# A decoder layer on one core: gated branch results summed by accumulating transfers, and a third staging buffer

## The chip, the core and the metric

The kernel runs on one core of a Trainium2 chip. Its engines are called here as in the profile: PE (TensorE, the matmuls), PEld (its weight loads), DVE (VectorE), ACT (ScalarE), POOL (GpSimd) and SP (SyncE, which issues nearly all transfers here). Each engine, and the queue of transfers that it issues, works through its own program in order. The metric is the device time of one execution in microseconds (us).

## The reference

One decoder layer over 1024 tokens of width 1024, all in float32: token mixing by three branches, then cross-attention into a memory of 256 rows, then an MLP with squared ReLU, and a final norm. What matters here is the end of the mixing:

```python
g = jax.nn.sigmoid(gates.reshape(bn, s_len, N_BRANCH, D_MODEL))
merged = (g[:, :, 0] * (od @ w_branch[l, 0])
          + g[:, :, 1] * (o_r @ w_branch[l, 1])
          + g[:, :, 2] * (o_l @ w_branch[l, 2]))
x = x + merged @ w_out[l]
```

`od`, `o_r` and `o_l` are the results of differential attention, retention and the recurrent unit. Each branch is a product of 1024x1024 by 1024x1024, gated by a sigmoid per element, and the three are added.

## The kernel before, in words

Every float32 operand of a matmul is split into two fp32r parts: `split` (L68) casts the high part on ACT (L70) and subtracts on DVE or POOL for the low part (L71). A product is then three matmuls per block, hi-hi, hi-lo, lo-hi (L59 to L61).

The large products run by Strassen's scheme in Winograd's form: seven products of half-size blocks in place of eight. `product` (L1104) makes one: it splits a weight block on ACT and DVE or POOL (tile `wu`), runs twelve matmuls into one of six PSUM buffers (tag `p`), and passes the sums that are complete on to `emit`. The sums of weights that the scheme needs are formed by `left` (L1064) on DVE in the staging tiles `st` and `sf`.

`branch` (L792) is called three times by `run` (L1302 to L1304), in the order retention, attention, recurrent; `order` counts the calls, `i` is the branch. In each call the first two pairs of weight units (p = 0, 1) run one after the other, and the last two (p = 2, 3) interleaved, product by product, so that the seven blocks of the activations come free one by one. While that goes on, `load_blocks` (L755) and `fill_block` (L770) refill each freed block with a block of the next branch's activations: two halves of 512 KB each are loaded into a staging tile `st2` (pool `bst`, two buffers, L1301; the profile calls it `st`) and split on ACT and DVE. In the third call there is no next branch: the merged sums are split into `mT` for the output projection, the first half of the rows read back from DRAM through the same staging buffers (L836), the second half straight from SBUF (L816).

`emit` (L800) handles one result tile of 128x512, 16 per call. It loads the gate tile `sg` (L803, four buffers; the profile calls it `sgb`), takes the sigmoid on ACT (L804), and from the second call on loads the running sum `pv` of the calls before (L807, three buffers). On DVE it adds the two parts of the product into `y` (L809, three buffers), multiplies by the gate (L810), and adds `pv` (L812). SP then stores `y` in a DRAM tensor (L814), one for each call (`self.acc`, L148), except for the last eight tiles of the third call.

The order of the instructions on each engine and queue is set by a scheduler when the program is built. A tile's buffer is taken again when its last reader is done; for `y` that reader is the transfer that stores it.

Of the kernel before, what the change touches and what calls it, by code (L numbers as in the profile page):

```python
# [9 lines left out]
F32 = mybir.dt.float32  # L10
F32R = mybir.dt.float32r
AF = mybir.ActivationFunctionType
ALU = mybir.AluOpType
# [4 lines left out]
P = 128  # L18
S = 1024
D = 1024  # L20
KT = 8
HB = 512
# [13 lines left out]
def f32(ap):  # L36
    return ap.bitcast(F32)
# [12 lines left out]
class Kernel:  # L50
# [85 lines left out]
    def setup(self):  # L136
        nc, tc, a, ctx = self.nc, self.tc, self.a, self.ctx
        self.const = ctx.enter_context(tc.tile_pool(name="const", bufs=1))
        self.small = ctx.enter_context(tc.tile_pool(name="small", bufs=4))
        self.stage = ctx.enter_context(tc.tile_pool(name="stage", bufs=3))  # L140
        self.wpool = ctx.enter_context(tc.tile_pool(name="wpool", bufs=4))
        self.dram = ctx.enter_context(tc.tile_pool(name="dram", bufs=1, space=DRAM))
        self.ps = ctx.enter_context(tc.tile_pool(name="ps", bufs=2, space=PSUM))
        dr = lambda n, shape: self.dram.tile(shape, F32, name=n)
        self.orT, self.odT, self.olT = dr("orT", [D, S]), dr("odT", [D, S]), dr("olT", [D, S])
        self.rows = dr("rows", [16, HB])
        self.onT, self.hTs = dr("onT", [D, S]), dr("hTs", [4, P, 4, HB])
        self.acc = [dr(f"acc{i}", [D, S]) for i in range(3)]  # L148
        self.oTs = [dr(f"oTs{i}", [4, P, 4, HB]) for i in range(3)]
        self.gsp = dr("gsp", [3 * D, S])  # L150
        self.h1 = self.dram.tile([8, 7, P, 2, HB], F32, name="h1")
        self.x2, self.x3 = dr("x2", [S, D]), dr("x3", [S, D])

        self.cm = cm = self.const.tile([P, 4, P], F32, name="cm")
        self.ident, self.ones, self.tril, self.negm = (cm[:, i, :] for i in range(4))
        self.onesr = self.const.tile([P, P], F32R, name="onesr")
        self.mhalf = self.const.tile([P, 8], F32, name="mhalf")
        nc.gpsimd.memset(self.mhalf, -0.5)
        self.vec = self.const.tile([P, NV], F32, name="vec")
        self.eps5 = self.const.tile([P, 1], F32, name="eps5")  # L160
        nc.gpsimd.memset(self.eps5, 1e-5)
        nc.scalar.activation(self.small.tile([P, 1], F32, tag="ss", name="ss", bufs=4), self.eps5, AF.Square)
        z = f32(self.wpool.tile([P, 2, D], F32R, tag="w", name="w"))[:, 0, 0:HB]
        nc.vector.memset(z, 0.0)
        for _ in range(3):
            nc.tensor.matmul(self.ps.tile([P, HB], F32, tag="mm", name="mm"), lhsT=z[:, 0:P], rhs=z, start=True, stop=True)
# [480 lines left out]
    def h_products(self):  # L647
# [64 lines left out]
        for p in range(2):  # L712
            run(p, 1)
            yield
# [8 lines left out]
        for k in self.BY_BLOCK[1:]:  # L723
            for p in range(2):
                run(p, k)
        for p in range(2, m - 2):
            for k in self.ORDER:
                run(p, k)
# [63 lines left out]
    def branch(self, order, i, right, bw, st, sps, nxt):  # L792

        nc, v = self.nc, self.nc.vector
        tile = lambda: st.tile([P, 2, HB], F32, tag="st2", name="st2")
        after, load = (None, None) if nxt is None else self.load_blocks(nxt, tile)
        mT = [[None, None], [None, None]]
        cs = [{} for _ in range(4)]

        def emit(n, j, x, y):  # L800
            rows, sl = slice(n * P, (n + 1) * P), slice(j * HB, (j + 1) * HB)
            sg = bw.tile([P, HB], F32, tag="sg", name="sgb", bufs=4)
            nc.sync.dma_start(sg, self.gsp[i * D + n * P:i * D + (n + 1) * P, sl])  # L803
            nc.scalar.activation(sg, sg, AF.Sigmoid)  # L804
            if order > 0:
                pv = bw.tile([P, HB], F32, tag="pv", name="pv", bufs=3)
                nc.sync.dma_start(pv, self.acc[order - 1][rows, sl])  # L807
            o = bw.tile([P, HB], F32, tag="y", name="y", bufs=3)
            v.tensor_tensor(o, x, y, op=ALU.add)  # L809
            v.tensor_tensor(o, o, sg, op=ALU.mult)  # L810
            if order > 0:
                v.tensor_tensor(o, o, pv, op=ALU.add)  # L812
            if nxt is not None or n < 4:
                nc.sync.dma_start(self.acc[order][rows, sl], o)  # L814
            else:
                self.split(mT[j][1][:, n % 4, :], o)  # L816

        def run(p, k):
            units = [self.a["w_br"][i * 8 + 2 * p + e] for e in range(2)]
            self.pair(p, k, cs[p], units, right, self.p6(sps), lambda e, j, x, y: emit(2 * p + e, j, x, y),  # L820
                      v if k in (6, 4) else nc.gpsimd)

        for p in range(2):
            for k in self.BY_BLOCK:
                run(p, k)
        for k in self.BY_BLOCK:
            for p in (2, 3):
                run(p, k)
            if nxt is not None:
                next(load)  # L830
            elif k in (1, 3):
                mT[k // 2][1] = self.block(self.slotA)
            elif k in (2, 7):
                j = 1 - k // 4
                mT[j][0] = self.block((self.slotB, self.slotA)[j])
                x = self.acc[2][:, j * HB:(j + 1) * HB].rearrange("(k p) c -> p k c", p=P)  # L836
                self.fill_block(mT[j][0], x, tile)
        return mT if nxt is None else after

# [445 lines left out]
    def run(self):  # L1285
        tc, nc, a = self.tc, self.nc, self.a
        pool = lambda name, bufs=1, side="right", **kw: tc.tile_pool(name=name, bufs=bufs, side=side, reuse_waits="tile", **kw)
        self.setup()
        with pool("slotA", bufs=4, side="left") as self.slotA:
# [5 lines left out]
            with pool("slotB", bufs=4) as self.slotB:  # L1295
                with pool("sps", space=PSUM) as sps:
                    with pool("sp") as self.sp:
                        self.sps = sps
                        for _ in self.hp:
                            pass  # L1300
                    with pool("bst", bufs=2) as st, pool("bw") as bw:  # L1301
                        right = self.branch(0, 1, self.right, bw, st, sps, 0)  # L1302
                        right = self.branch(1, 0, right, bw, st, sps, 2)
                        mT = self.branch(2, 2, right, bw, st, sps, None)  # L1304
# [94 lines left out]
```

## Time and profile before

| | |
|---|---|
| median of 3 runs | 2452.02 us (2450.01 to 2455.37) |
| the profiled execution | 2450.84 us, span 2448.9 us, mean granted clock 0.985 |
| PE busy | 2312.1 us, 94% of the span |
| DVE, ACT, POOL busy | 1885.1 (77%), 1043.4 (43%), 997.8 us (41%) |
| transfers | 338.27 MB, mean 138 GB/s |
| the merge of the three branches | some 1262 to 1536 us of the span |

The span is from the first to the last instruction. Busy times overlap between engines. The granted clock is TensorE's, as a share of 2.4 GHz. A wait is put down to what ended it last. In the rows below, "x2" means that two like instructions are merged, and their time is the sum.

### The profile page before, as it was taken

What the parts mean: (1) busy time and instruction counts of PE and PEld (TensorE: products, weight loads), DVE (VectorE), ACT (ScalarE), POOL (GpSimd) and SP (SyncE); (2) the same over time, 40 slices, a digit from 0 to 9 for tenths busy, and PEclk for the clock granted to TensorE, in tenths of its full rate; (3) what the DMA queues carried; (4) which work ended last, traced back from release to release, by engine and by line L of the source; (5) the groups of instructions that cost most, each with busy time, mean ns of one, the idle gap of its engine ahead of it and who ended that gap; (6) DMA issues with size and microseconds to landing.
All of it is one profiled execution on the core that took longest, in us unless ns stands there. A gap on an engine that the chain in (4) does not pass through costs nothing.

```text
span 2448.9 us, 31204 instructions
## 1 busy us (share of the span) xinstructions
PE 2312.1 (94%) x11132; PEld 1901.4 (78%) x11132; DVE 1885.1 (77%) x2920; ACT 1043.4 (43%) x1823; POOL 997.8 (41%) x644
## 2 busy tenths in 40 slices
PE   9999999999999989899998988999989999899996
PEld 7888878888887867677877766788768888778884
DVE  7677387877797787897787888345788888788888
ACT  5444355555555444545244444135432222343333
POOL 1122212221215434455422214034155555698787
PEclk9999999999999999999999989999999999999999
DMA  4222222222225345443576785343324443734431
GB/s 172 80 86 70 65 61 70 66 61 65 61 51 186 123 153 189 144 159 131 193 257 224 249 281 183 112 163 104 113 83 166 152 160 135 276 136 173 160 137 73
DMA packets 137258, 338.27 MB, mean 138 GB/s; under 512 B 17152, under 2 KB 27393, under 8 KB 137104
## 3 DMA queue, kind: packets, MB, share of 16 engines
q1 hardware_dynamic: 136528, 334.44, 41.5%
q8 instruction: 89, 1.46, 0.3%
q10 hardware_dynamic: 576, 1.84, 0.2%
q14 instruction: 65, 0.53, 0.1%
HBM read 229.21 MB, written 98.63 MB: 134 GB/s over the span
## 4 chain that ended last, share of the span: by engine, by line
PE 51%; DVE 20%; DMA 11%; issue 8%; POOL 5%; ACT 4%; SPq 0%; DVEq 0%; POOLq 0%; ACTq 0%
PE ps L61 7%; PE ps L59 7%; PE ps L60 7%; POOL wu L71 3%; PE psq L59 2%; PE psq L61 2%; PE psq L60 2%; PE sc L458 2%; PE psk L61 2%; DVE block L71 2%; PE psk L60 2%; PE psk L59 2%; DVE acc L1199 2%; DMA st<-oTs 1%; PE psv L60 1%
## 5 line engine op out<-in xcount | busy, mean ns | idle before, releaser
L59 PE MATMUL ps<-block,wu 128*128 128x512 f32 x1428 | 567.6, 398 | 48.3 <-DVE sf L1126 16.1
L61 PE MATMUL ps<-block,wu 128*128 128x512 f32 x1428 | 564.8, 396 | 22.3 <-DVE wu L71 15.2
L60 PE MATMUL ps<-block,wu 128*128 128x512 f32 x1428 | 560.7, 393 | 0.2 <-DVE block L71 0.2
L71 POOL TENSOR_TENSOR wu<-st,wu 128x512 fp32r<-128x512 f32 x144 | 226.0, 1577 | 385.4 <-ACT wu L70 341.8
L59 PEld LDWEIGHTS ps<-block,wu 128*128 128x128 f32 x1428 | 271.0, 190 | 111.9 <-ACT wu L70 29.0
L61 PEld LDWEIGHTS ps<-block,wu 128*128 128x128 f32 x1428 | 270.5, 189 | 90.5 <-DVE wu L71 18.6
L60 PEld LDWEIGHTS ps<-block,wu 128*128 128x128 f32 x1428 | 270.8, 190 | 60.0 <-DVE block L71 1.1
L70 ACT CAST wu<-st 128x512 fp32r<-128x512 f32 x240 | 141.3, 618 | 156.7 <-DVE st L1066 63.1
L59 PE MATMUL ps<-wu,hu 128*128 128x512 f32 x448 | 177.2, 395 | 16.9 <-DVE acc L1199 14.1
L71 POOL TENSOR_TENSOR w<-st,w 128x1024 fp32r<-128x1024 f32 x50 | 124.7, 2505 | 161.3 <-ACT w L70 161.3
L61 PE MATMUL ps<-wu,hu 128*128 128x512 f32 x448 | 174.7, 392 | 3.8 <-DVE hu L71 3.8
L60 PE MATMUL ps<-wu,hu 128*128 128x512 f32 x448 | 175.5, 392 | 0.0
L1199 DVE TENSOR_TENSOR acc<-acc,ps 128x512 f32<-128x512 f32 x216 | 137.8, 677 | 20.5 <-PE ps L61 20.0
L71 POOL TENSOR_TENSOR wu<-sf,wu 128x512 fp32r<-128x512 f32 x63 | 116.3, 1859 | 53.5 <-ACT wu L70 51.7
L71 DVE TENSOR_TENSOR hu<-sth,hu 128x1024 fp32r<-128x1024 f32 x56 | 121.1, 2167 | 20.4 <-ACT hu L70 19.9
L466 ACT ACTIVATE p<-sc,mx 128x256 f32<-128x256 f32 (+7 forms) x128 | 94.8, 741 | 69.9 <-DVE mx L463 50.2
L71 DVE TENSOR_TENSOR wu<-st,wu 128x512 fp32r<-128x512 f32 x96 | 90.1, 954 | 35.1 <-ACT wu L70 35.1
L59 PEld LDWEIGHTS ps<-wu,hu 128*128 128x128 f32 x448 | 84.6, 189 | 40.8 <-DVE acc L1199 12.2
L61 PEld LDWEIGHTS ps<-wu,hu 128*128 128x128 f32 x448 | 84.7, 189 | 22.9 <-DVE hu L71 5.1
L59 PE MATMUL psk<-block,w 128*128 128x512 f32 x256 | 102.2, 399 | 0.0
L61 PE MATMUL psk<-block,w 128*128 128x512 f32 x256 | 101.4, 396 | 0.0
L60 PE MATMUL psk<-block,w 128*128 128x512 f32 x256 | 101.3, 396 | 0.0
(389 smaller groups left out, 5638.5 us busy)
## 6 DMA issues: line engine op xcount, KB each, us to landing
sth<-h SPq DMA_DIRECT2D x56, 512.0 KB, 9.5
st<-in_w SPq DMA_DIRECT2D x32, 512.0 KB, 4.3
h<-hab SPq DMA_DIRECT2D x32, 512.0 KB, 2.8
w<-in_w SPq DMA_DIRECT2D x8, 2048.0 KB
sgb<-gsp SPq DMA_DIRECT2D x48, 256.0 KB, 4.6
gsp<-l SPq DMA_DIRECT2D x44, 256.0 KB, 4.0
acc<-y SPq DMA_DIRECT2D x40, 256.0 KB, 4.1
st<-in_w_br SPq DMA_DIRECT2D x18, 512.0 KB, 5.9
```

The lines of the kernel that those rows point to most:

```text
L59: nc.tensor.matmul(ps, lhsT=lhs.hi, rhs=rhs.hi, start=start, stop=False)
L60: nc.tensor.matmul(ps, lhsT=lhs.hi, rhs=rhs.lo, start=False, stop=False)
L61: nc.tensor.matmul(ps, lhsT=lhs.lo, rhs=rhs.hi, start=False, stop=stop)
L70: ins = self.nc.scalar.copy(dst.hi, src)
L71: self.lo_ins = (lo_engine or self.nc.vector).tensor_tensor(dst.lo, src, f32(dst.hi), op=ALU.subtract)
L458: nc.tensor.matmul(sc[:, b * HB:b * HB + e], lhsT=qt[:, c, part, cols], rhs=k[b][:, c, 0:e], start=part == 0, stop=part == 1)
L466: nc.scalar.activation(p[:, 0:n], sc[:, 0:n], AF.Exp, bias=mx, accum_out=l)
L1199: eng.tensor_tensor(acc[k][:, st, :], acc[k][:, st, :], x if isinstance(x, bass.AP) else acc[x][:, st, :], op=ALU.add)
```

## The change

The three DRAM tensors for the running sum become one. In the first call SP stores each result there as before. In the second call, and for the first eight results of the third, a transfer issued by POOL adds the result to what stands in DRAM (`accum_op=ALU.add`); the load of `pv` and the addition on DVE are gone there. The last eight results of the third call load the sum and add it as before. The gate tile has three buffers in place of four, `pv` two in place of three, and the staging pool of `fill_block` three in place of two; the room in SBUF is the same.

```diff
-        self.acc = [dr(f"acc{i}", [D, S]) for i in range(3)]
+        self.acc = dr("acc", [D, S])
...
-            sg = bw.tile([P, HB], F32, tag="sg", name="sgb", bufs=4)
+            sg = bw.tile([P, HB], F32, tag="sg", name="sgb", bufs=3)
             nc.sync.dma_start(sg, self.gsp[i * D + n * P:i * D + (n + 1) * P, sl])
             nc.scalar.activation(sg, sg, AF.Sigmoid)
-            if order > 0:
-                pv = bw.tile([P, HB], F32, tag="pv", name="pv", bufs=3)
-                nc.sync.dma_start(pv, self.acc[order - 1][rows, sl])
+            acc, last = self.acc[rows, sl], nxt is None and n >= 4
+            if last:
+                pv = bw.tile([P, HB], F32, tag="pv", name="pv", bufs=2)
+                nc.sync.dma_start(pv, acc)
             o = bw.tile([P, HB], F32, tag="y", name="y", bufs=3)
             v.tensor_tensor(o, x, y, op=ALU.add)
             v.tensor_tensor(o, o, sg, op=ALU.mult)
-            if order > 0:
+            if not last:
+                if order == 0:
+                    nc.sync.dma_start(acc, o)
+                else:
+                    nc.gpsimd.dma_start(acc, o, accum_op=ALU.add)
+            else:
                 v.tensor_tensor(o, o, pv, op=ALU.add)
-            if nxt is not None or n < 4:
-                nc.sync.dma_start(self.acc[order][rows, sl], o)
-            else:
                 self.split(mT[j][1][:, n % 4, :], o)
...
-                x = self.acc[2][:, j * HB:(j + 1) * HB].rearrange("(k p) c -> p k c", p=P)
+                x = self.acc[:, j * HB:(j + 1) * HB].rearrange("(k p) c -> p k c", p=P)
...
-                    with pool("bst", bufs=2) as st, pool("bw") as bw:
+                    with pool("bst", bufs=3) as st, pool("bw") as bw:
```

PE's program is the same before and after. On the other engines the scheduler moves instructions in this stage; three places follow. Numbers are buffer numbers, and an arrow points from what is read to what is written.

SP's queue in the second call, while p = 0 and p = 1 run (before; `acc_79` is the running sum being written, `acc_78` the one read):

```order
L814 DMA acc_79<-y 128x512
L807 DMA pv<-acc_78 128x512
L1077 DMA st<-in_w_br 128x1024
L774 DMA st_13026<-olT 128x2x512
L774 DMA st_13030<-olT 128x2x512
L803 DMA sgb<-gsp 128x512
```

And with the change, at the end of the first call and the start of the second:

```order
L774 DMA st_12659<-oTs_79 128x1024
L774 DMA st_13000<-olT 128x2x512
L814 DMA acc<-y 128x512 x3
L803 DMA sgb<-gsp 128x512 x3
L1080 DMA st<-in_w_br 128x1024
L803 DMA sgb<-gsp 128x512
L1080 DMA st<-in_w_br 128x1024
L774 DMA st_13004<-olT 128x2x512
L774 DMA st_13054<-olT 128x2x512
```

The first load of the next branch's block (`st_13000<-olT`) now stands ahead of the last stores of the first call, so three are issued ahead and not two, and no store or load of the sum is left between the loads of weights, gates and blocks.

POOL's queue, from the end of the second call to p = 1 of the third (before), where `wu` are weight splits:

```order
L71 TENSOR_TENSOR wu_13466<-sf_8246,wu_13466 128x512
L71 TENSOR_TENSOR wu_13577<-st_13528,wu_13577 128x512
L71 TENSOR_TENSOR wu_13577<-sf_8246,wu_13577 128x512
L71 TENSOR_TENSOR wu_13608<-sf_8246,wu_13608 128x512
L71 TENSOR_TENSOR wu_13755<-st_13688,wu_13755 128x512
```

The same place with the change:

```order
L71 TENSOR_TENSOR wu_13413<-sf_8244,wu_13413 128x512
L816 DMA acc_78<-y_13251 128x512
L816 DMA acc_78<-y_13282 128x512
L816 DMA acc_78<-y_13305 128x512
L816 DMA acc_78<-y_13357 128x512
L71 TENSOR_TENSOR wu_13512<-st_13466,wu_13512 128x512
L71 TENSOR_TENSOR wu_13512<-sf_8244,wu_13512 128x512
L71 TENSOR_TENSOR wu_13543<-sf_8244,wu_13543 128x512
L816 DMA acc_78<-y_13432 128x512
L816 DMA acc_78<-y_13440 128x512
L816 DMA acc_78<-y_13462 128x512
L816 DMA acc_78<-y_13504 128x512
```

The transfers stand in groups of two to four between the splits; the results of p = 0 of the third call (from `y_13432` on) come behind the three splits of p = 1.

DVE in the third call, p = 0 and the first result of p = 1 (before: L809 adds, L810 multiplies, L812 adds the running sum, L1066 forms the weight sums that the splits of p = 1 read):

```order
L809 TENSOR_TENSOR y_13523<-ps1_13505,sf_8246 128x512
L812 TENSOR_TENSOR y_13498<-y_13498,pv_13496 128x512
L810 TENSOR_TENSOR y_13523<-y_13523,sgb_13518 128x512
L1066 TENSOR_TENSOR st_13528<-sf_8246,st_13528 128x512
L812 TENSOR_TENSOR y_13523<-y_13523,pv_13521 128x512
L809 TENSOR_TENSOR y_13568<-ps1_13550,sf_8246 128x512
L1066 TENSOR_TENSOR st_13528<-st_13528 128x512
```

With the change (the lines are L810, L811 and L1069 there):

```order
L1069 TENSOR_TENSOR st_13466<-st_13466 128x512
L1129 TENSOR_TENSOR sf_8244<-ps1_13398,sf_8244 128x512
L1069 TENSOR_TENSOR sf_8244<-st_13616 128x512
L1131 TENSOR_TENSOR sf_8244<-ps1_13383,sf_8244 128x512
L71 TENSOR_TENSOR wu_13543<-st_13466,wu_13543 128x512
L1069 TENSOR_TENSOR st_13616<-st_13614,st_13616 128x512
L810 TENSOR_TENSOR y_13432<-ps1_13416,sf_8244 128x512
L1134 TENSOR_TENSOR sf_8244<-ps1_13416,sf_8244 128x512
L811 TENSOR_TENSOR y_13432<-y_13432,sgb_13429 128x512
L810 TENSOR_TENSOR y_13440<-ps1_13367,sf_8244 128x512
```

The weight sums of p = 1 (`st_13528` before, `st_13466` now) moved ahead of the results of p = 0. The add into `y_13504`, p = 1's first result, waits until `y_13432` has been added to DRAM, since they share one of the three buffers.

## Rows read from the trace of the kernel before

**Rows 1.** Busy time in stretches of 10 us of the merge: the stretch and its length, then for PE, PEld, DVE, ACT and POOL the busy us and the number of instructions in brackets, the granted clock, the mean busy share of the transfer engines, and GB/s.

```profile
1310.00:1320.00 10.00, 8.44 (x37) 6.57 (x35) 6.91 (x7) 5.98 (x8) 1.82 (x1) 1.00 0.94 301
1320.00:1330.00 10.00, 3.56 (x9) 2.82 (x10) 7.96 (x10) 4.18 (x5) 0.00 (x0) 0.67 0.67 226
...
1350.00:1360.00 10.00, 10.00 (x45) 8.18 (x45) 9.96 (x16) 4.89 (x8) 0.73 (x1) 1.00 1.00 348
...
1400.00:1410.00 10.00, 5.28 (x24) 3.98 (x22) 7.22 (x10) 5.72 (x9) 1.81 (x1) 0.94 0.87 328
1410.00:1420.00 10.00, 6.65 (x18) 5.24 (x19) 8.71 (x13) 4.94 (x8) 0.67 (x1) 0.55 0.78 273
...
1440.00:1450.00 10.00, 7.57 (x27) 5.75 (x27) 8.85 (x15) 3.12 (x5) 0.00 (x0) 0.83 0.94 297
1450.00:1460.00 10.00, 6.38 (x28) 4.99 (x27) 9.32 (x16) 3.36 (x6) 0.29 (x1) 1.00 0.87 304
1460.00:1470.00 10.00, 10.00 (x37) 7.59 (x36) 6.72 (x7) 5.05 (x10) 4.38 (x3) 0.83 0.81 253
...
1520.00:1530.00 10.00, 3.33 (x10) 2.02 (x9) 10.00 (x10) 4.08 (x5) 6.56 (x4) 0.74 0.60 197
1530.00:1540.00 10.00, 7.20 (x20) 5.56 (x20) 6.86 (x9) 1.24 (x2) 2.43 (x1) 0.57 0.75 234
```

**Rows 2.** Waits in 1255 to 1540 us: the engine and line that waited, what ended the wait, us in total, times, longest.

```profile
ACT sgb L804 <- DMA sgb<-gsp: 44.4, 22, 7.2
...
PE ps L59 <- DVE sf L1126: 16.1, 2, 8.1
...
PE ps L59 <- ACT wu L70: 3.6, 1, 3.6
...
PE ps L61 <- DVE wu L71: 2.4, 1, 2.4
```

**Rows 3.** Timeline of 1316 to 1333 us: start, us, engine, line, operation, and in brackets the idle time before it with what ended it. The first and the last of five casts of a staged half block, and the first one's subtraction on DVE.

```profile
1316.97 1.05 ACT L70 CAST block<-st 128x1024 fp32r<-128x1024 f32 x1 [0.89 <-DMA st<-odT]
...
1318.05 1.23 DVE L71 TENSOR_TENSOR block<-st,block 128x1024 fp32r<-128x1024 f32 x1 [2.08 <-ACT block L70]
...
1331.99 1.05 ACT L70 CAST block<-st 128x1024 fp32r<-128x1024 f32 x1 [3.75 <-DMA st<-oTs]
```

**Rows 4.** Waits of SP's own queue of transfers in 1255 to 1540 us, columns as in the second group. L814 stores a result, L807 loads the running sum.

```profile
SPq L814 <- DVE y L810: 32.1, 14, 9.8
SPq L814 <- DVE y L812: 19.7, 21, 2.5
...
SPq L807 <- DVE y L812: 8.9, 4, 3.2
```

**Rows 5.** Transfers in 1300 to 1350 us: packets and MB with the mean rate, then issues by what is written and read, count, KB each, median us from issue to landing.

```profile
DMA packets 5083, 12.53 MB, mean 251 GB/s; under 512 B 509, under 2 KB 509, under 8 KB 5082
...
st<-odT SPq DMA_DIRECT2D x4, 512.0 KB, 6.4
acc<-y SPq DMA_DIRECT2D x8, 256.0 KB, 2.1
```

**Rows 6.** The instructions that write or read tile y, over the run: least, median and greatest ns, first and last start. L814 is SP's issue of the plain store.

```profile
L814 SPq DMA_DIRECT2D acc<-y x40: 319/320/1281, 1274.6 to 1480.0; - x40
L812 DVE TENSOR_TENSOR y<-y,pv x32: 674/679/2896, 1352.2 to 1534.2; 128x512 f32<-128x512 f32 x32
```

**Rows 7.** The page's list of transfer issues over the run, columns as in the fifth group.

```profile
sgb<-gsp SPq DMA_DIRECT2D x48, 256.0 KB, 4.6
...
acc<-y SPq DMA_DIRECT2D x40, 256.0 KB, 4.1
...
pv<-acc SPq DMA_DIRECT2D x32, 256.0 KB, 4.4
```

**Rows 8.** Timeline of DVE: single adds (L809) and multiplications (L810) of results, columns as in the third group.

```profile
1383.85 0.68 DVE L810 TENSOR_TENSOR y<-y,sgb 128x512 f32<-128x512 f32 x1
1397.02 0.68 DVE L809 TENSOR_TENSOR y<-ps,sf 128x512 f32<-128x512 f32 x1
1419.85 0.68 DVE L809 TENSOR_TENSOR y<-ps,sf 128x512 f32<-128x512 f32 x1
1441.77 0.68 DVE L809 TENSOR_TENSOR y<-ps,sf 128x512 f32<-128x512 f32 x1
1450.82 0.68 DVE L810 TENSOR_TENSOR y<-y,sgb 128x512 f32<-128x512 f32 x1
1456.23 0.68 DVE L809 TENSOR_TENSOR y<-ps,sf 128x512 f32<-128x512 f32 x1
1508.63 0.69 DVE L809 TENSOR_TENSOR y<-ps,sf 128x512 f32<-128x512 f32 x1 [1.14 <-PE ps L61]
1530.15 0.68 DVE L809 TENSOR_TENSOR y<-ps,sf 128x512 f32<-128x512 f32 x1
```

**Rows 9.** Timeline of POOL: weight splits, columns as in the third group.

```profile
1389.52 2.55 POOL L71 TENSOR_TENSOR wu<-st,wu 128x512 fp32r<-128x512 f32 x2 [8.54 <-ACT wu L70]
...
1459.71 1.28 POOL L71 TENSOR_TENSOR wu<-st,wu 128x512 fp32r<-128x512 f32 x1 [31.66 <-ACT wu L70]
1460.95 3.43 POOL L71 TENSOR_TENSOR wu<-sf,wu 128x512 fp32r<-128x512 f32 x2
```

**Rows 10.** The instructions on tile sgb over the run, columns as in the sixth group: the sigmoid of the gate.

```profile
L804 ACT ACTIVATE sgb<-sgb x48: 613/632/635, 1270.5 to 1518.9; 128x512 f32<-128x512 f32 x48
```

## The prediction

> **What bounds the kernel now.** I read the table of busy time first, then the same table in stretches of 10 us over the merge of the three branches, then the waits of that stage, then single rows of the timeline. The table of the whole run says that TensorE (PE) is the bound: busy 94% of the span, so the change can only win where PE stands still. The stretches [rows 1] say where. A stretch in which PE waits for nothing holds 45 matmuls of this shape (1350 to 1360), which is 0.222 us each. Below that lie 1310 to 1330 with 37 + 9 matmuls, 44 short of 90, or 9.8 us lost; 1400 to 1420 with 24 + 18, or 10.7 us; 1440 to 1470 with 27 + 28 + 37, 43 short, or 9.6 us; and 1520 to 1540 with 10 + 20, or 13.3 us. Together 43.4 us. Part of it is the clock: after PE stood still, the granted clock was 0.67 and 0.55 on average in two of these stretches, between the two levels of 1.0 (2.4 GHz) and 0.5 (1.2 GHz). The counts hold that cost already.
>
> The waits [rows 2] give the reasons. Twice PE waits some 8 us for line L1126, that is for a PSUM buffer that VectorE (DVE) empties late. What held it up is the ring that loads the next branch's blocks: each cast of a staged half block waits for its load. Five of these casts, the first and the last of them in [rows 3], stand at 1316.97 to 1331.99, four steps in 15.0 us, 3.76 us a load. PE uses 14 products of 12 matmuls per 14 loads, 37.3 us, so it wants a load each 2.67 us. The third stop, at 1440 to 1460, has DVE busy 8.85 and 9.32 us of 10 [rows 1] and ends with PE waiting 2.4 us for a DVE weight split and 3.6 us for an ACT cast [rows 2]; ACT itself waited 44.4 us in this stage for gates (sgb) that landed late, and the load of a gate stands in SP's queue behind stores and loads that wait for DVE [rows 4]. The last stop belongs to the tail of the third branch and to the output projection behind it.
>
> **The change, part by part.** PE's program is the same, row for row; only other engines and queues move.
>
> *Third staging buffer.* With two buffers at 3.76 us a load, one turn of the ring takes 7.5 us. Bound below: nothing, if the DMA engines can't go faster. Bound above: the whole of the first two stops, 9.8 + 10.7 us, since 7.5 / 3 is 2.5 us, less than the 2.67 that PE wants. Between them: 1300 to 1350 moved 12.53 MB at 251 GB/s [rows 5], and one stretch reached 348 [rows 1], so there is room, but not much: at 348 GB/s the same bytes take 36 us. I take the slower landing in that stretch, 6.4 us [rows 5], for each load of three in flight; with cast 1.05 and subtraction 1.23 [rows 3], and an issue of 0.32 [rows 6], a turn is 9.0 us, 3.0 us a load, 0.33 more than PE wants, and 14 loads leave 4.7 us of a stop of some 10. So **-5 us** for each of the two stops, -10 together. The queue order agrees: a third load is issued ahead.
>
> *24 additions and 24 loads gone.* An addition is 0.68 us of DVE when alone [rows 6], so 24 are 16.3 us. Nearly all lies beside PE's work and buys nothing. On the path is the third stop: seven results of the second and third branch are added between 1419.85 and 1441.77 [rows 8], and their seven additions (4.8 us) stand ahead of the split that PE waits for; four more (2.7 us) stand ahead of the late cast. That is 7.5 us at most. SP's queue loses 48 transfers, whose waits for DVE were 32.1 + 19.7 + 8.9 us [rows 4], a part of them with the gates' loads behind. I take **-5 us** of the third stop's 9.6; the ends are 0 and -9.6.
>
> *24 accumulating transfers on POOL's queue.* No row shows POOL issue a transfer or a transfer add. Issue: between SP's 0.32 us for the plain store [rows 6] and POOL's 1.28 us for its cheapest operation on the same tile [rows 9]. I take 1.3, since it is POOL that makes it; 24 are 31 us of an engine that is busy 4.4 us or less of each stretch up to 1470 [rows 1]. Landing: not under the plain store's 2.1 [rows 5], and not over a load and a store one after the other, 4.4 + 4.1 = 8.5 us [rows 7], unless both are slow (6.4 twice, 12.8). It reads two tiles and writes one, so the nearest row is the load of two tiles' bytes, 6.4 us [rows 5]. The Trainium skill (page "DMA: Bandwidth & Descriptors", section "Anatomy of one DMA — SWDGE (gpsimd) path") prices a transfer from this queue at 2.0 us plus its bytes at 436 GB/s, 2.6 us for a tile. No run here shows one, and a plain store of that size took 4.1 us in the median, so the page looks low here; by its estimate the next term would be 0 and the sum 2437.
>
> *What waits for them.* The result tile y has three buffers, so the add of a result waits until the third result before it has landed. In a burst: six steps from 1419.85 to 1441.77, 3.65 us a result, 10.95 us for three. With two DVE operations (1.36), the issue (1.3) and 6.4 a turn is 9.1: no wait. But POOL is served in order, and its queue now has weight splits ahead of some transfers. The split pair at 1389.52 ends at 1392.07 [rows 9]; the result multiplied at 1383.85 [rows 8] stands behind it and lands at 1392.07 + 1.3 + 6.4 = 1399.8; the add that needs its buffer stood at 1397.02: 2.8 us late. In the third branch three splits end at 1464.4 [rows 9] ahead of the result multiplied at 1450.82; if they stay that late it lands at 1472, and the add that was at 1456.23 [rows 8] waits 15.9 us with all of DVE behind it. If they come sooner, which the new order of DVE allows because the sums they need stand earlier, it waits nothing. PE's lead hides short waits of DVE. I take **+3 us**, the size of the one wait that I can place; the ends are 0 and +16.
>
> *At nothing.* Three gate buffers in place of four: a turn is 4.6 us landing [rows 7], 0.63 sigmoid [rows 10], two DVE operations and the issue, about 7 us or 2.3 a result, and DVE's pace of 3.65 in a burst covers it; if DVE went faster than 2.3, the gates would set the pace. Two pv buffers in place of three: only the last eight results use them, and a turn of 4.4 landing, 0.4 issue and two DVE operations, 6.2 us or 3.1 a result, is under the tail's own pace (five steps from 1508.63 to 1530.15, 4.3 a result [rows 8]); without that cover it is the tail that grows. The tail keeps its instructions, and its 13.3 us stay.
>
> **Sum.** The profiled execution took 2450.84 us (span 2448.9 and 1.9 around it), 1.2 under the median of the runs, 2452.02. 2450.84 - 10 - 5 + 3 = 2438.8, on the median **2440 us**. The measurement can tell 0.2% of it, 4.9 us, from no change.
>
> **Rivals.**
>
> *A: the ring of y becomes the wait (slower).* A landing beyond 10.95 - 1.36 - 1.3 = 8.3 us makes a burst longer than before. At 12.8 a turn is 15.5 us, 5.2 a result: +1.5 us for each of six, 9 us; and at the places where splits stand ahead of transfers, two as above and two like them, 6.4 us more each, 25.6, of which PE's lead hides about half. 2440 + 9 + 13 = 2462 us. For it: only three buffers, and POOL's one queue for splits and transfers. Against: even a load and a store in sequence is 8.5 us.
>
> *B: the transfers are the limit (no change).* The DMA engines were busy 0.67 to 1.00 of the stretches named [rows 1], and an accumulation still reads what the load read. Then the third buffer gives 0, the additions' -5 and the ring's +3 stay, and the hold-ups on transfers take these 2 too: 2452 us. The Trainium skill (page "Collectives: The Full Stack", section "The bandwidth ceiling: the fold count and why AG ≠ RS ≠ AR") says the same of a reduction by transfers: it needs two source reads, and ran at half the rate of a copy. No run here shows it yet.
>
> *C: all three stops vanish.* 2.5 us a load is enough and POOL's splits come early: -9.8 - 10.7 - 9.6 gives 2422 us. Against: the DMA share of 0.94 at 1310 and at 1440.
>
> **How the numbers follow.** Forecast 0.43, A 0.24, B 0.20, C 0.13. Faster by over 0.2%: the forecast nearly whole (0.41), C, and a fifth of B (0.04): 0.58. Within 0.2%: 0.12 of B, 0.02 of the forecast, 0.02 of A: 0.16. Slower: most of A and the rest of B, 0.26. The range: C's worse half begins at 2425, and the better half of A ends at 2461; outside are half of C (0.06) and somewhat under half of A (0.10).
>
> **What would show it.** In the changed profile: 24 transfers from POOL; their landing near 6.4 us (A if over 8.3, and then DVE's add of the result waits for a transfer acc<-y); block loads nearer 3.0 than 3.76 us apart and the waits of PE on L1126 at some 4 us each, or 8 still (B), or gone (C); the stop at 1440 to 1470 halved; the tail as before. I am wrong if a new wait of DVE on the accumulation stands at the head of PE's waits, or if the tail, which I left at nothing, moves.

## The result: slower by 0.3%, and the profile after

The changed kernel took 2459.7 us in the median of 7 runs (2456.6 to 2464.5), the kernel before 2453.4 beside it (7 runs, 2450.0 to 2457.4): a ratio of 1.0031, with an interval of 1.0019 to 1.0043. The forecast was 2440. The time lies in the range given, near its upper end, and on the side that got 0.26. The profiled execution took 2457.33 us with a span of 2455.5, 6.6 us longer than the span before.

The stretches of 10 us of the changed kernel, columns as in [rows 1]:

```profile
1310.00:1320.00 10.00, 7.89 (x35) 6.14 (x33) 7.46 (x7) 5.30 (x8) 2.34 (x1) 1.00 0.92 316
1320.00:1330.00 10.00, 3.15 (x8) 2.50 (x9) 9.65 (x15) 5.39 (x8) 0.12 (x1) 0.61 0.85 299
1330.00:1340.00 10.00, 10.00 (x40) 8.12 (x39) 9.92 (x13) 5.77 (x8) 4.50 (x3) 0.87 0.70 233
1400.00:1410.00 10.00, 7.00 (x31) 5.41 (x29) 7.80 (x9) 3.75 (x6) 3.77 (x4) 1.00 0.95 255
1410.00:1420.00 10.00, 0.00 (x0) 0.02 (x1) 8.36 (x11) 5.80 (x8) 0.00 (x0) 0.55 0.93 333
1420.00:1430.00 10.00, 9.98 (x34) 8.07 (x35) 10.00 (x14) 5.16 (x7) 3.55 (x4) 0.77 0.81 253
1440.00:1450.00 10.00, 9.90 (x44) 7.82 (x43) 9.90 (x16) 3.88 (x6) 2.62 (x3) 1.00 0.91 212
1450.00:1460.00 10.00, 10.00 (x46) 8.21 (x45) 7.63 (x10) 3.75 (x7) 4.87 (x4) 1.00 0.40 120
1460.00:1470.00 10.00, 10.00 (x46) 8.18 (x45) 4.50 (x8) 2.69 (x5) 2.45 (x3) 1.00 0.98 215
1470.00:1480.00 10.00, 4.97 (x22) 3.73 (x20) 7.29 (x10) 2.76 (x6) 2.12 (x2) 0.96 0.40 102
1480.00:1490.00 10.00, 9.75 (x31) 7.82 (x32) 5.83 (x9) 2.02 (x5) 5.12 (x5) 0.69 0.55 104
1520.00:1530.00 10.00, 5.41 (x21) 3.54 (x19) 10.00 (x8) 3.35 (x5) 6.55 (x3) 0.85 0.56 168
1530.00:1540.00 10.00, 7.57 (x23) 6.04 (x24) 9.97 (x10) 3.26 (x5) 5.16 (x2) 0.63 0.65 203
1540.00:1550.00 10.00, 5.99 (x18) 4.44 (x18) 2.51 (x4) 0.50 (x1) 0.00 (x0) 0.71 0.56 204
```

And of the kernel before, stretches that [rows 1] leaves out:

```profile
1330.00:1340.00 10.00, 10.00 (x44) 8.21 (x43) 8.96 (x14) 3.79 (x4) 0.00 (x0) 0.98 0.77 258
1420.00:1430.00 10.00, 10.00 (x45) 8.24 (x44) 10.00 (x12) 5.07 (x7) 4.59 (x3) 1.00 0.75 227
1470.00:1480.00 10.00, 10.00 (x45) 8.22 (x45) 9.98 (x17) 1.73 (x3) 1.30 (x1) 1.00 0.34 103
1480.00:1490.00 10.00, 10.00 (x46) 8.29 (x45) 6.61 (x6) 4.86 (x9) 5.95 (x4) 1.00 0.78 239
1540.00:1550.00 10.00, 10.00 (x45) 8.22 (x44) 1.66 (x4) 1.15 (x2) 0.56 (x1) 1.00 0.21 84
```

Counted as in the prediction, in matmuls short of 45 per 10 us (a stretch with more counts as 45), the first stop is 52 short in 1310 to 1340, 11.6 us (45 short before, 10.0 us); the second 70 short in 1400 to 1430, 15.6 us (10.7 before); the third, 9.6 us before, is gone; and a new one stands at 1470 to 1490, 37 short, 8.2 us (nothing before). The tail is 73 short in 1520 to 1550, 16.2 us, where the prediction counted 13.3. Counted from 1500 on, where 1500 to 1520 hold 38 and 45 matmuls (32 and 44 before), it is 17.8 us, and 16.4 before. So 9.6 us were won at the third stop, 8.2 came back 20 us later, and the first stop, the second and the tail grew by 1.6, 4.9 and 1.4. That is 6.5 us in all, and the span grew by 6.6. The granted clock fell in the stops and stayed low behind them: with not one matmul in 1410 to 1420, it was 0.55 there and 0.77 in the next stretch.

The waits in 1255 to 1540 us, columns as in [rows 2]:

```profile
ACT sgb L804 <- DMA sgb<-gsp: 87.2, 35, 7.8
...
PE ps L59 <- DVE sf L1129: 23.3, 3, 13.0
...
DVE y L810 <- DMA acc<-y: 5.9, 4, 2.3
```

Against [rows 2], the wait that the profile puts down to gates doubled (44.4 to 87.2 us); all of ACT's idle time before sigmoids, whatever is said to have ended it, went from 64.9 to 88.8 us. PE's wait for DVE grew from 16.1 to 23.3 us. DVE's own wait for accumulations, the sign of rival A, is 5.9 us in all.

The new stop is read from the timelines of ACT and PE, columns as in [rows 3], and from two pieces of the chain of waits that leads to it (start, us, what):

```profile
1475.90 0.63 ACT L804 ACTIVATE sgb<-sgb 128x512 f32<-128x512 f32 x1 [5.19 <-DMA sgb<-gsp]
1476.44 1.12 ACT L70 CAST wu<-st 128x512 fp32r<-128x512 f32 x2
1479.61 1.14 ACT L70 CAST wu<-st 128x512 fp32r<-128x512 f32 x2 [2.05 <-DVE st L1069]
...
1480.25 0.76 PE L59 MATMUL ps<-block,wu 128*128 128x512 f32 x1 [5.28 <-ACT wu L70]
```

```profile
1461.95 7.00 DMA sgb<-gsp
...
1471.58 4.22 DMA sgb<-gsp
```

The casts of weights (`wu`) stand in ACT's program behind the sigmoid of a gate that has not landed. ACT waits 5.19 us for it; DVE's split and its next weight sum wait for the cast, the following cast for that sum, and PE, 5.28 us, for that cast. The gate's load itself landed in 4.22 us, no slower than the median before (4.6). It was issued late, when DVE had multiplied by an earlier gate and so freed the buffer, and the chain goes back over that to a gate that took 7.00 us. So one slow load is handed on, through the programs of ACT and DVE and the ring of gates, to the next.

Last, the transfers of 1345 to 1500 us, columns as in [rows 5]; q0 is the queue of the accumulating transfers, q1 all of SP's:

```profile
q1 hardware_dynamic: 9933, 24.08, 48.1%
q0 software_dynamic: 3456, 6.29, 26.3%
...
acc<-y POOLq DMA_DIRECT2D x24, 256.0 KB, 6.9
```

24 accumulations took 26.3% of 155 us of all sixteen transfer engines, 1.70 us each. On SP's queue 256 KB take 0.81 us (48.1% of 155 us for 24.08 MB). So an accumulation takes about what a load and a store take together. It landed in 6.9 us; the prediction had 6.4.

### The profile page after: what moved, and what is told of

It is laid out like the page before. It is cut to its first block, busy times and chain, and to the rows that moved or that the text cites. A ratio compares the mean times of both kernels' runs of the same rounds, so it can differ in the third digit from the quotient of the medians.

```text
span 2455.5 us, 31180 instructions
## 1 busy us (share of the span) xinstructions
PE 2325.5 (95%) x11132; PEld 1913.2 (78%) x11132; DVE 1865.5 (76%) x2896; ACT 1043.0 (42%) x1823; POOL 1010.0 (41%) x668
## 3 DMA queue, kind: packets, MB, share of 16 engines
q0 software_dynamic: 3456, 6.29, 1.7%
## 4 chain that ended last, share of the span: by engine, by line
PE 52%; DVE 19%; DMA 11%; issue 8%; POOL 6%; ACT 3%; SPq 0%; POOLq 0%; DVEq 0%; ACTq 0%
PE ps L59 7%; PE ps L61 7%; PE ps L60 7%; POOL wu L71 3%; PE psq L59 2%; PE psq L61 2%; PE psq L60 2%; DMA sgb<-gsp 2%; PE sc L458 2%; PE psk L61 2%; PE psk L60 2%; PE psk L59 2%; DVE block L71 1%; DVE acc L1202 1%; DMA st<-in_w_br 1%
## 5 line engine op out<-in xcount | busy, mean ns | idle before, releaser
L59 PE MATMUL ps<-block,wu 128*128 128x512 f32 x1428 | 572.9, 401 | 47.4 <-DVE sf L1129 26.9
L59 PEld LDWEIGHTS ps<-block,wu 128*128 128x128 f32 x1428 | 274.4, 192 | 111.1 <-issue 35.4
L61 PEld LDWEIGHTS ps<-block,wu 128*128 128x128 f32 x1428 | 273.7, 192 | 85.5 <-DVE wu L71 14.3
L60 PEld LDWEIGHTS ps<-block,wu 128*128 128x128 f32 x1428 | 274.1, 192 | 61.1 <-DVE block L71 1.0
L59 PE MATMUL ps<-wu,hu 128*128 128x512 f32 x448 | 177.9, 397 | 15.4 <-DVE acc L1202 12.4
L1202 DVE TENSOR_TENSOR acc<-acc,ps 128x512 f32<-128x512 f32 x216 | 137.6, 677 | 19.8 <-PE ps L61 19.5
L59 PEld LDWEIGHTS ps<-wu,hu 128*128 128x128 f32 x448 | 84.9, 189 | 39.9 <-DVE acc L1202 11.8
L59 PE MATMUL psk<-block,w 128*128 128x512 f32 x256 | 101.6, 397 | 0.0
```

Source lines behind the costliest of these rows:

```text
L59: nc.tensor.matmul(ps, lhsT=lhs.hi, rhs=rhs.hi, start=start, stop=False)
L60: nc.tensor.matmul(ps, lhsT=lhs.hi, rhs=rhs.lo, start=False, stop=False)
L61: nc.tensor.matmul(ps, lhsT=lhs.lo, rhs=rhs.hi, start=False, stop=stop)
L1202: eng.tensor_tensor(acc[k][:, st, :], acc[k][:, st, :], x if isinstance(x, bass.AP) else acc[x][:, st, :], op=ALU.add)
```

## The experiments

Each was timed beside the kernel before, whose median was 2446.5 to 2448.0 us in these runs; 0.1% is 2.4 us. Theories at first: the gate ring (G), the accumulating transfers on POOL's queue (P), the third staging buffer (S).

**four_gates** (changed kernel, `sg` back to 4), **four_results** (changed kernel, `y` to 4):

```diff
-            sg = bw.tile([P, HB], F32, tag="sg", name="sgb", bufs=3)
+            sg = bw.tile([P, HB], F32, tag="sg", name="sgb", bufs=4)
```

> The changed kernel with its gate ring back at four buffers (2 KB per partition more). Theory G, the gate ring: the changed kernel lost its time where ScalarE waits for a gate whose buffer came free late (1400 to 1430, 15.6 us of TensorE against 10.7; 1470 to 1490, 8.2 against 0). Then both shrink: 4.9 and some 6 us less, about 2449 us, and ScalarE's wait for gates falls from 87 us to 50 or less. Theory P, the accumulating transfers on GpSimd's queue: no change, 2459. Theory S, the third staging buffer (block loads bunch and slow each other): no change, 2459.

> The changed kernel with a fourth buffer for results (y), so that the addition of a result waits for the accumulation four results back. Theory P: the waits of VectorE for accumulations (5.9 us) go, and the hold-up behind them: 2453 to 2456. Theories G and S: no change, 2459; a gate's load still waits for the multiplication three results back.

Measured 1.0023 (1.0014 to 1.0032) and 1.0042 (1.0029 to 1.0055); **change_again** gives the reference in this series:

> The changed kernel itself, for its ratio beside the other kernels of this study: 1.003, as measured first (1.0019 to 1.0043).

It measured 1.0036 (1.0024 to 1.0048). A fourth result buffer, in the changed kernel's order, brings nothing clear of the noise, so the ring of `y` is not the wait. A fourth gate buffer brings some 0.13% (1.0036 to 1.0023; the intervals overlap), and ACT's wait for gates is 83.4 us, not under 50: theory G, as I had put it, fell.

**accumulate_alone** (changed kernel with `bst` 2, `sg` 4, `pv` 3) and **buffers_alone** (kernel before with `bst` 3, `sg` 3, `pv` 2):

> The accumulating transfers alone: two staging buffers, four gate buffers and three pv buffers as before the change. Theory G: the first two stops as before (10.0 and 10.7 us), the third smaller by the additions that are gone, 0 to 9.6 us: 2444 to 2453, about 2448 us. Theory P: as slow as the changed kernel or slower, 2458 or more. Theory S: 2448, since the third staging buffer isn't there.

> The kernel before with the change's buffers alone: three for staging, three for gates, two for pv; loads and additions of sums stay. Theory G: the third stop (9.6 us) stays and the gates' lateness comes on top, 5 to 10 us: 2458 to 2463. Theory P: the third staging buffer's gain without its cost, 2443 to 2453. Theory S: slower than before by a few us, 2455 to 2460.

Measured 1.0052 (1.0040 to 1.0064) and 1.0042 (1.0029 to 1.0055). Each half of the change loses alone, and together they lose no more than either, far from the sum of both (0.94%): they interact. But the halves are not quite those of the change: in buffers_alone all 32 loads of sums go through two `pv` buffers, in the changed kernel only eight do.

**plain_store_same_order** and **plain_store_from_sp** take accumulate_alone apart:

```diff
-                    nc.gpsimd.dma_start(acc, o, accum_op=ALU.add)
+                    nc.gpsimd.dma_start(acc, o)      # plain_store_same_order
+                    nc.sync.dma_start(acc, o)        # plain_store_from_sp
```

> The accumulating transfers alone (buffers as before the change, 1.0052 of the kernel before), with each accumulating transfer replaced by a plain store at the same place of the same queue; every engine's order stays. The sums of the second and third branch are left out, so the transfer reads one tile and not two. Theory T, the transfer itself (an accumulation takes the transfer engines about twice as long as a store and slows the loads beside it, those of gates above all): back to 0.998 to 1.001 of the kernel before, and the landing of acc<-y falls from 6.9 us to 4 or less. Theory O, the order (without the sums' loads and additions the scheduler puts gates, stores and blocks into an order that waits more): 1.004 to 1.006, as with accumulation.

> As the run before, but the plain stores are issued by SP, as all stores of results were before the change: no transfer of POOL, no load and no addition of sums (they are left out), buffers as before the change. It bounds what the removal of loads and additions can bring. Theory T: 0.995 to 0.998 (the third stop of 9.6 us gone). Theory O: 1.002 or more. If POOL's queue is what costs (a transfer waits behind splits), this is faster than the run before by 0.3% or more.

Measured 0.9996 (0.9986 to 1.0006) and 0.9982 (0.9973 to 0.9992). The first differs from accumulate_alone in the transfer alone, and is 0.56%, 13.7 us, faster: theory T. Every engine's instructions stand in one and the same order in the two traces. The waits (1255 to 1560 us) and transfers (1345 to 1500 us) of accumulate_alone:

```profile
ACT sgb L804 <- DMA sgb<-gsp: 74.4, 29, 7.2
...
PE ps L59 <- DVE sf L1129: 20.5, 2, 11.7
...
PE ps L59 <- ACT wu L70: 7.5, 3, 3.0
...
q0 software_dynamic: 3456, 6.29, 25.8%
...
acc<-y POOLq DMA_DIRECT2D x24, 256.0 KB, 7.0
```

And of plain_store_same_order:

```profile
ACT sgb L804 <- DMA sgb<-gsp: 49.1, 22, 6.2
...
PE ps L59 <- ACT wu L70: 11.1, 3, 7.7
...
PE ps L59 <- DVE sf L1129: 7.6, 1, 7.6
...
q0 software_dynamic: 1920, 6.29, 10.3%
...
acc<-y POOLq DMA_DIRECT2D x24, 256.0 KB, 4.3
```

The bytes counted are the same; the time on the transfer engines is 2.5 times as long (25.8 against 10.3%: 1.67 us a tile against 0.67). DVE, whose next result needs the buffer, waits no longer for the transfer itself (3.3 against 3.5 us); SP does, 11.8 us at the end, which the next two runs take up. Who waits for other loads waits longer. The profile shifts some of these waits from one name to another between the two runs, so they are taken together: ACT's idle time before sigmoids is 78.5 against 69.0 us, and PE's waits at L59 for DVE and ACT are 28.0 against 18.7. An accumulation also takes POOL longer to issue, but PE's wait for POOL's splits is 0.5 against 0.2 us. One place shows the way from transfer to PE. With accumulations (of the two merged loads, the first counts):

```profile
1367.54 16.16 SPq L803 DMA_DIRECT2D sgb<-gsp  x2
...
1375.79 0.63 ACT L804 ACTIVATE sgb<-sgb 128x512 f32<-128x512 f32 x1 [2.94 <-DMA sgb<-gsp]
1376.32 1.12 ACT L70 CAST wu<-st 128x512 fp32r<-128x512 f32 x2
...
1380.15 0.47 PE L59 MATMUL ps<-block,wu 128*128 128x512 f32 x1 [1.87 <-ACT wu L70]
```

And with plain stores, where PE waits for nothing here:

```profile
1365.46 16.19 SPq L803 DMA_DIRECT2D sgb<-gsp  x4
...
1369.84 0.63 ACT L804 ACTIVATE sgb<-sgb 128x512 f32<-128x512 f32 x1 [0.91 <-DVE wu L71]
```

The sigmoid came 8.2 us after its gate's load was issued in the one, 4.4 us in the other. This is the place where the two differ most; most gates that stand first in a group of loads came as soon in both.

**accumulate_second_call** and **accumulate_third_call** accumulate 16 or 8 of the 24, in the same order:

```diff
-                    nc.gpsimd.dma_start(acc, o, accum_op=ALU.add)
+                    nc.gpsimd.dma_start(acc, o, **({} if nxt is None else dict(accum_op=ALU.add)))
```

> As accumulate_alone, in the same order on every engine, but only the 16 results of the second call are accumulated; the 8 of the third call are stored plainly (their sum is left out). accumulate_alone stood at 1.0052 and the same order with 24 plain stores at 0.9996. Theory C (each accumulation costs by the time it takes of the transfer engines, which the loads of gates and blocks beside it lose): 16 of 24 parts, 0.9996 + 0.0037 = 1.0033. Theory W (the cost is the end: SP's queue stands 11.8 us for two accumulations before it may read the sums back): 1.000.

> The other way round, same order: only the 8 results of the third call are accumulated, the 16 of the second are stored plainly (left out of the sum). Theory C: 8 of 24 parts, 0.9996 + 0.0019 = 1.0015. Theory W: the whole cost, 1.005.

Measured 1.0029 (1.0018 to 1.0040) and 1.0009 (0.9999 to 1.0020): over 0.9996 that is 0.33% for 16 and 0.13% for 8, against 0.56% for 24. The cost goes with their number, some 0.5 us each, although the eight alone are not clear of the noise. SP's wait at the end is not it: it is there whole in accumulate_third_call (12.4 us).

**third_staging_alone** (kernel before with `bst` 3 and `pv` 2), **three_gates_alone** and **five_gates_before** (kernel before with `sg` 3 and 5), **four_results_before** (kernel before with `y` 4):

```diff
-                    with pool("bst", bufs=2) as st, pool("bw") as bw:
+                    with pool("bst", bufs=3) as st, pool("bw") as bw:
```

> The kernel before with three staging buffers and two pv buffers; four gate buffers, loads and additions of sums as before. As the prediction put it, -5 us at each of the first two stops: 0.996 (10 us of 2450). Theory G2 (of the three buffer edits, the gates' cost what buffers_alone lost): 0.996 to 1.000. Theory S (the third staging buffer makes block loads bunch and land later, and the gates' loads with them): 1.002 to 1.005.

> The kernel before with three gate buffers in place of four, nothing else. The prediction put it at nothing: 1.000. Theory G2: it carries the whole 0.4% of buffers_alone: 1.003 to 1.005. Theory S: 1.000 to 1.001.

> The kernel before with five gate buffers, nothing else. Theory G (the gates' ring sets ScalarE's waits): where a fourth buffer was worth 0.31%, a fifth is worth some of the 44 us that ScalarE still waits for gates: 0.997 to 0.999. If the fourth buffer was the last that mattered: 1.000.

> The kernel before with a fourth buffer for results, nothing else: the addition of a result waits for the store four results back and not three. VectorE hardly waits for stores before, so 1.000; if the scheduler uses it to move stores behind gates' loads, 0.998.

Measured 1.0009 (0.9998 to 1.0019), 1.0031 (1.0018 to 1.0044), 1.0023 (1.0013 to 1.0033), 1.0007 (0.9996 to 1.0018). A fifth gate buffer can only loosen the ring, and is slower all the same. Both edits of the gate ring move the scheduler's order: compared line by line, 20 of the 827 transfers in SP's list stand elsewhere with five gates and 21 with three, and DVE's and ACT's programs move as well; `y` 4 moves none of SP's. So three_gates_alone doesn't show that the ring's wait costs 0.3%; an order that the scheduler happens to choose is worth as much. Which of the two it is there stays open.

The third staging buffer takes away ACT's wait for block loads. ACT's wait for the main group of them in 1255 to 1560 us, before and in third_staging_alone:

```profile
ACT block L70 <- DMA st<-oTs: 25.9, 15, 3.7
```

```profile
ACT sgb L804 <- DMA sgb<-gsp: 57.6, 25, 6.9
...
DVE y L812 <- DMA pv<-acc: 7.7, 5, 2.8
...
ACT block L70 <- DMA st<-oTs: 4.5, 7, 1.7
```

But other loads took their place. On the chain of waits of third_staging_alone (start, us, what) stand a load of a gate at the first stop and loads of the running sum before the second stop and before the third, which is at 1430 to 1450 here:

```profile
1310.49 6.83 DMA sgb<-gsp
```

```profile
1382.70 4.66 DMA pv<-acc
...
1420.06 4.68 DMA pv<-acc
```

This run does not show the third staging buffer by itself. It has two `pv` buffers for all 32 loads of sums, DVE's wait of 7.7 us for them is new, and the order of SP's transfers changed too (30 of 827 stand elsewhere). A kernel before with three staging and three `pv` buffers was not run.

**change_with_two_staging** and **four_gates_plain_store** (four_gates with the plain store) show the staging buffer where most loads of sums are gone:

> The changed kernel with two staging buffers, as before the change; three gate buffers, two pv buffers and the accumulating transfers stay. If the parts add up (accumulation +0.52%, three gates +0.31%): 1.008 of the kernel before. If the third staging buffer is what pays for a part of the slower transfers: 1.005 to 1.009, in any case clearly above the changed kernel's 1.003. If the third staging buffer does as little here as alone (1.0009): 1.003.

> As four_gates (accumulation, three staging buffers, four gate buffers: 1.0023), in the same order, with each accumulating transfer replaced by a plain store (the sums are left out). If accumulation costs the same with three staging buffers as with two (0.0056): 0.997, and the third staging buffer is then worth 0.3% in this order with or without it. If the third staging buffer pays only because accumulation makes loads slow: 1.000, a cost of accumulation of 0.002.

Measured 1.0068 (1.0056 to 1.0080) and 0.9959 (0.9945 to 0.9973). With accumulations the third buffer is worth 0.29% (accumulate_alone to four_gates, which also has two `pv` in place of three) or 0.32% (change_with_two_staging to change_again), with plain stores 0.37% (0.9996 to 0.9959). So its gain does not depend on the accumulation, which costs 0.64% here, again in one and the same order. That it depends on the loads of sums being gone fits third_staging_alone but is not shown, since that run has the shorter `pv` ring and its own order.

Where PE gained and lost can be counted in these runs as above, from the same table of 10 us stretches, in us. Each stop is taken over the stretches in which it falls in that run; the tail is what is lost from 1490 on. The changed kernel and change_again, one and the same kernel, agree within 1.4 us at each place.

| run | first stop | second | third | 1470 to 1490 | tail |
|---|---|---|---|---|---|
| kernel before | 10.0 | 10.7 | 9.6 | 0 | 16.4 |
| third_staging_alone | 11.8 | 9.6 | 12.4 | 0 | 15.3 |
| plain_store_from_sp | 8.4 | 6.0 | 9.6 | 0 | 14.7 |
| plain_store_same_order | 10.4 | 9.3 | 6.2 | 0 | 19.8 |
| accumulate_alone | 11.1 | 13.3 | 6.2 | 3.3 | 21.3 |
| four_gates_plain_store | 10.7 | 11.8 | 0 | 0 | 14.2 |
| four_gates | 8.2 | 14.2 | 1.6 | 6.0 | 14.7 |

In both orders the accumulation makes the second stop longer and brings the stop at 1470 to 1490. And in both, with the third staging buffer and the order that comes with it, the third stop and the tail get shorter, by 11 to 12 us together, while the first two stops together stay within 3 us of what they were.

**gates_from_pool_before** (kernel before, `sg` loaded by POOL):

```diff
-            nc.sync.dma_start(sg, self.gsp[i * D + n * P:i * D + (n + 1) * P, sl])
+            nc.gpsimd.dma_start(sg, self.gsp[i * D + n * P:i * D + (n + 1) * P, sl])
```

> The kernel before with the loads of gates issued by GpSimd in place of SP; all else as before. SP's queue stood 38.5 us for the buffers of gates, with loads of blocks behind; that goes. Theory Q (SP's queue, where loads of gates stand in front of loads of blocks and behind them, is what makes both late): 0.997 to 0.999. Against it: GpSimd's queue then stands for VectorE with weight splits behind it, and 1.003 or more if those come late for TensorE.

Measured 1.0052 (1.0039 to 1.0065); ACT's wait for gates is 86.0 us, as in the changed kernel, and loads of sums land in 6.6 us in 1345 to 1500 us, against 4.4 before:

```profile
ACT sgb L804 <- DMA sgb<-gsp: 86.0, 35, 6.9
...
pv<-acc SPq DMA_DIRECT2D x25, 256.0 KB, 6.6
```

Theory Q, as I had put it, fell. The run does not show that SP's queue is harmless: POOL itself stood 75.5 us for DVE at these loads, and the order changed. No kernel that computes the whole sum beat the one before.

## Why the prediction was wrong, by its own steps

One path leads through the runs from the kernel before to the changed one, and its parts add up by construction; 0.1% is 2.45 us. Only the third row compares two kernels in one and the same order. The others hold also what a new order of the scheduler's is worth; in five_gates_before a looser ring and its new order cost 0.23%, 5.6 us.

| step | forecast, us | measured, us | from |
|---|---|---|---|
| 24 additions and loads gone | -5 | -4.4 | plain_store_from_sp |
| POOL's queue and the ring of y | +3 | +3.4 | to plain_store_same_order |
| a transfer that adds, in place of a store | 0 | +13.7 | to accumulate_alone |
| third staging buffer (and two pv) | -10 | -7.1 | to four_gates |
| three gate buffers | 0 | +3.2 | to change_again |
| sum | -12 | +8.8 (0.36%) | |

The measured differences of the second and the fifth row lie within what the intervals leave open; those of the third and the fourth don't.

*24 additions and 24 loads gone*: right in size, by luck as far as the traces show. The gain was forecast at the third stop, which plain_store_from_sp has as before, 9.6 us; there the second stop above all got shorter. In the changed kernel the third stop went whole and not half, but only runs that also have the third staging buffer show it gone or nearly so.

*Third staging buffer*: near its size, and luck again. It was counted as 5 us at each of the first two stops, from block loads 3.0 us apart. These two stops did not get 10 us shorter in any run; in the changed kernel they are 11.6 and 15.6 us, and its waits of PE at the heads of them (L1126 before, L1129 now) are 9.0 and 13.0 us, where the prediction had 4. What the buffer gave came at the third stop and in the tail. Alone, with the shorter `pv` ring, it brought nothing (1.0009).

*24 accumulating transfers, what waits for them*: **this step failed.** The landing (6.4 forecast, 6.9) was near, the issue (1.3 forecast, 0.87) shorter, and the ring of `y` waits 5.9 us in all, so rival A is not what happened. But the prediction asked only who waits for an accumulation, and not what it takes from the transfers beside it; that stood at nothing, without a reason. In one and the same order, an accumulation in place of a plain store took 1.0 us more of all sixteen engines and made gates beside it land later (8.2 us against 4.4 in the place shown); ACT, which serves its program in order, held PE's weight casts behind sigmoids, and the kernel took 13.7 us more. That the engines' time is the reason is what the count of 8, 16 and 24 fits, not a thing shown by itself. A price could be had: rival B says that an accumulation still reads what the load read, and a load and a store are 0.8 us each on these engines. B used it to take a gain away; it should have stood in the sum as a cost. The Trainium skill's sentence that the prediction gave there (page "Collectives: The Full Stack", section "The bandwidth ceiling: the fold count and why AG ≠ RS ≠ AR": a reduction reads two sources and goes at half the rate) agrees in direction with the 1.67 us against 0.67 measured here, which is 2.5 times. The estimate of 2.6 us from the Trainium skill's price (page "DMA: Bandwidth & Descriptors", section "Anatomy of one DMA — SWDGE (gpsimd) path") was too low for both kinds beside other transfers: 4.3 us plain, 6.9 accumulating.

*Three gate buffers at nothing*: the cover named was DVE's pace in a burst. The ring's length is not what made ACT wait so much more for gates: with four buffers it still waits 83.4 us (87.3 in change_again). What the fourth buffer is worth beside accumulations, 3.2 us, is at the edge of what the intervals tell; the zero was not far off.

*The tail, left as it was*: 13.3 us became 16.2 (16.4 and 17.8 when counted from 1500), which the prediction had named as a sign that it is wrong; its other sign, a wait of DVE on accumulations at the head, did not come. In the two pairs of the table the tail is 5.6 and 6.6 us shorter with the third staging buffer, so it was not to be left out; what made it longer in the changed kernel was not taken apart.

One thing stays open. The load and the store that an accumulation replaces took as much time of the engines (0.79 us each before, from 75.1% of 155 us for 38.49 MB) as it does, and yet accumulate_alone is 12.5 us slower than the kernel before. So the 13.7 us are what an accumulation costs against a plain store; why it costs more than a store and a load together is not shown. That SP's transfers come one after the other in the order that the scheduler gave, while POOL's run beside them, would explain it, and gates_from_pool_before, slower by the same amount with the same bytes, would fit. But both runs also have another order than the kernel before, and no run moves a transfer from one queue to the other in one and the same order.

## What to carry to other kernels

A transfer that adds in place saves an engine's addition and a queue's load, not the transfer engines' time: price it at a load and a store of transfer time, and ask which late load beside it PE will wait for. Check a gain at the place where it was forecast, and not by its size alone: two terms came out near their size here from other stops than the ones they were counted at. Ask of each wait that goes which one takes its place, as loads of gates and sums took the place of the block loads here. And where a scheduler sets the order, a buffer more or less moves instructions: take one edit's 0.2% as the order's until a run in the same order says otherwise.

## What the runs showed of the hardware

An accumulating transfer of 128x512 from SBUF to DRAM took 144 packets (3456 for 24) and 1.67 us of all sixteen engines, a plain one from the same queue 80 packets (1920 for 24) and 0.67 us. POOL needed 870 ns to issue the first in the changed kernel and 540 ns to issue the second in four_gates_plain_store; SP issues a plain store in 320 ns [rows 6]:

```profile
L816 POOL DMA_DIRECT2D acc<-y x24: 862/870/1160, 1350.7 to 1486.3; - x24
```

```profile
L816 POOL DMA_DIRECT2D acc<-y x24: 539/540/777, 1345.5 to 1470.7; - x24
```
